# Moving the forget-gate log gathers of a two-layer hybrid decoder into the SSD tiles

## The chip, the cores and the metric

One Trainium2 chip, one core. The metric is the device time of one execution of the program in microseconds (us). Three executions of the kernel before took 2384.43, 2384.25 and 2366.11 us, median 2384.25 us. A further execution was recorded by the profiler and took 2400.34 us; its trace spans 2398.7 us from the first to the last instruction.

## The reference

The program computes one inference step of a two-layer decoder on 576 tokens: one new prompt of 512 tokens and eight running sequences with eight new tokens each. All numbers are 32-bit floats. In each layer a token mixer runs three branches on the same input, merges them with sigmoid gates, and projects:

```
u, q, k, v, fg, z, xbc, dt = split(x @ w_in)          # and three gates
logf  = log_sigmoid(fg + b)                           # forget gate, 8 heads
y_s5  = diagonal complex state space (u)
y_fox = softmax(q k' + cumulated logf differences) v  # forgetting attention
y_ssd = Mamba-2 state space (conv(xbc), dt)
out   = (g0*(y_s5 @ w0) + g1*(y_fox @ w1) + g2*(y_ssd @ w2)) @ w_o
```

For the running sequences the attention also reads a cache of 256 past tokens, held in pages of 128 tokens. For each sequence a page table names two pages, so 16 pages in all. The cache has keys, values (512 floats per token each) and the forget-gate logs `cache_logf` (8 floats per token). The score of a past token gets the sum of the forget-gate logs of all later past tokens, so the cached logs of all 16 pages are needed, once per layer, by the attention of the running sequences. After the mixer, layer 0 has a dense feed-forward part (width 2816) and layer 1 eight experts of which each token uses two.

## The kernel before

Everything is spread over five engines that run side by side, each in its own fixed order: TensorE (PE) for matrix products, VectorE (DVE) and ScalarE (ACT) for elementwise work, GpSimd (POOL) for elementwise work and for issuing transfers, and SyncE (SP), which issues the weight loads. A planner at build time puts the instructions of PE, DVE, ACT and POOL in order by a simulated timeline: an instruction goes to its engine once its inputs are ready there, and of several that are ready the one that stands first in the program. So work that stands late in the program is pulled forward into an engine's idle time if nothing holds it. SP's order is the order of the program (line 56). `tc.issue_after(x)` adds one constraint: what stands in the block comes behind `x` on `x`'s engine.

Every dense product is made exact by splitting each factor into a high and a low part: ACT rounds a weight tile (`wh`, line 97), DVE subtracts (`wl`, line 106), and PE multiplies three times (lines 294 to 296).

The order of the program in layer 0 (lines 1585 to 1598) is: load and transpose the input, issue the 16 log gathers of layer 0 (`gather_logs(0)`, line 1593), start the S5 constants (`s5_steps`, line 349), project `u`, then `mixer(0)`: the convolution, `ssd(0)`, keys, queries and values with the prompt's attention (`kqv_fox`), the S5 scan, and `fox_sample(0)`, the attention of the running sequences. Then come merge, output projection and the feed-forward part; `gather_logs(1)` stands in that part (line 1604), behind the S5 constants of layer 1.

`gather_logs` issues one indirect transfer per page from POOL (line 972). Each takes 128 rows of 8 floats into `lfp[:, i, :]`, with row numbers from `pgi`. The tile `lfp` has two buffers, one for each layer, so nothing makes the gathers of layer 1 wait for layer 0. They are read in `fox_sample` alone (line 1001): pair `bp` of sequences copies four of the 16 slices into `lq`, the left factor of a product.

`ssd(l)` walks over five tiles of tokens (four of 128 and one of 64) with a `front` and a `back` each. In a front, POOL loads the convolved input (`xc`, line 1158), multiplies `xd` by a decay into `xdd` (line 1169), and builds the masked decay matrices `ma` (line 1184; in layer 0 POOL builds the first of each pair and DVE the second). PE takes `ma` at line 1185 and `xdd` at line 1215. POOL's queue also holds, in the same stretch, the transfers of the prompt's attention (`kT`, `qT`, `vt`, `cb`, lines 890 to 900) and the subtractions for `kq` (line 859).

Of the kernel before, what the change touches and what calls it, by code (L numbers as in the profile page):

```python
# [8 lines left out]
F32 = mybir.dt.float32  # L9
# [10 lines left out]
P = 128  # L20
# [25 lines left out]
def decoder_step(ctx, tc, A, O):  # L46
    nc = tc.nc
    act, dve, pool, pe, sp = nc.scalar, nc.vector, nc.gpsimd, nc.tensor, nc.sync
    consts = ctx.enter_context(tc.tile_pool(name="consts", bufs=1))
    wk = ctx.enter_context(tc.tile_pool(name="wk", bufs=2))  # L50
# [9 lines left out]
    def U(tag, shape, dt=F32, name="u"):  # L60
        return cur["pool"].tile(shape, dt, name=name, tag=tag, bufs=cur["bufs"][tag])
# [4 lines left out]
    def SW(name="s"):  # L66
        return U("S", [P, 512], F32, name)

    def phase(name, **bufs):
        st_ = ExitStack()  # L70
        cur["pool"] = st_.enter_context(tc.tile_pool(name=name, bufs=1, reuse_waits="tile"))
        cur["bufs"] = bufs
        return st_
# [10 lines left out]
    def PX(name="px"):  # L84
        return ps.tile([P, 512], F32, name=name, tag="px", bufs=2)

    def PA(name="pa"):
        return ps.tile([P, 512], F32, name=name, tag="pa", bufs=1)
# [7 lines left out]
    def cp(out, in_):  # L96
        return act.activation(out, in_, AF.Copy)  # L97

    def mul(e, out, a, b):
        return e.tensor_tensor(out, a, b, op=OP.mult)  # L100

    def add(e, out, a, b):
        e.tensor_tensor(out, a, b, op=OP.add)  # L103
# [16 lines left out]
    def bc(ap, axis, n):  # L120
        u = ap.unsqueeze(axis)
        shp = list(u.shape)
        shp[axis] = n
        return u.to_broadcast(shp)
# [96 lines left out]
    pgi = []  # L221
# [9 lines left out]
    def tr(out, in_, n):  # L231
        pe.transpose(out, in_, ident[:n, :n])  # L232
# [3 lines left out]
    def x_dma(i):  # L236
        n = P if i < 4 else 64
        src = A["x_prompt"][0, i * P:(i + 1) * P, :] if i < 4 else A["x_sample"].rearrange("b t d -> (b t) d")
        xts[i] = xt = U("A", [P, D], name="xt")
        sp.dma_start(out=xt[:n], in_=src)  # L240

    def x_tr(i):
        n = P if i < 4 else 64
        xt = xts[i]
        for k0 in (0, 4):
            pt = (PX, PF)[k0 // 4]("xp")
            pv = pt.rearrange("p (k t) -> p k t", k=4)
            for k in range(4):
                tr(pv[:, k, :n], xt[:n, (k0 + k) * P:(k0 + k + 1) * P], n)
            s = slice(i * P, i * P + n)  # L250
            split(xh[:, k0:k0 + 4, s], xl[:, k0:k0 + 4, s], pv[:, :, :n])
# [6 lines left out]
    def wload(src, c0, ncol, kt, after=None):  # L258
        if WB["body"]:
            raw = [WB["pool"].tile([P, 4, P], F32, name="wb", tag="wb", bufs=2) for a in range(2)]  # L260
            for a in range(2):
                sp.dma_start(out=raw[a], in_=src[a * 512:a * 512 + 512, c0:c0 + P].rearrange("(k p) c -> p k c", p=P))
            return raw
        raw = wt_([P, 8, P], F32, "wr")
        i_ = sp.dma_start(out=raw[:, :kt, :ncol], in_=src[:, c0:c0 + ncol].rearrange("(k p) c -> p k c", p=P))
        if after is not None:
            tc.add_manual_dep(i_.ins, after.ins.name, mybir.DependencyInfo(
                mybir.DependencyClass.Sync, mybir.DependencyReason.DATA), reason="gather first")
        return raw
# [459 lines left out]
    def u_proj(l, hooks=(), first=()):  # L729
        us = {}  # L730

        def ev_u(j, h, o):
            if h == 0:
                us[j] = wk.tile([P, 8, 72], F32, name="us", tag="xp", bufs=4)
            ov = o.rearrange("p (k s) -> p s k", s=8)
            for a, b, k0 in (((0, 36, 8),), ((0, 28, 44), (28, 36, 0)))[h]:
                cp(us[j][:, :, k0:k0 + b - a], ov[:, :, a:b])
            if h == 1:
                i_ = pool.dma_start(out=UD[l][j * P:(j + 1) * P].rearrange("p (s k) -> p s k", s=8), in_=us[j])
                if j == 0:  # L740
                    S["late"] = i_
            for at, f in hooks:
                if (j, h) == at:
                    f()
        colblocks(A["w_in"][l], C_U, 512, 8, X, ev_u, by_half=True, first=first)
# [217 lines left out]
        for u_, r_ in pend:  # L963
            back(*u_, r_)

    lfps = {}

    def gather_logs(l):
        lfps[l] = lfp = wk.tile([P, 16, 8], F32, name="lfp", bufs=2)
        clf = A["cache_logf"].rearrange("l n p h -> (l n p) h")  # L970
        for i in range(16):
            pool.indirect_dma_start(out=lfp[:, i, :], out_offset=None, in_=clf,
                                    in_offset=bass.IndirectOffsetOnAxis(ap=pgi[l][:, i:i + 1], axis=0))

    def fox_sample(l):
        kS, qS, vn = S["kS"], S["qS"], S["vn"]
        lf = S["lf"]
# [97 lines left out]
    def conv(l, w_in):  # L1075
# [41 lines left out]
        for j0 in (0, 4):  # L1117
# [5 lines left out]
            pool.dma_start(out=O[7][l, 0, :, j0 * P:j0 * P + 512], in_=t_[0:3])  # L1123
            pool.dma_start(out=O[14][l].rearrange("b j c -> (b j) c")[:, j0 * P:j0 * P + 512], in_=t_[3:27])

    def ssd(l):
        lf = S["lf"]
        adt = wk.tile([P, 5, 8], F32, name="adt", bufs=1)
# [21 lines left out]
        v8 = lambda a: a.rearrange("p (h d) -> p h d", h=8)  # L1150
        st = {}

        def front(i):
            n = P if i < 4 else 64
            ts = slice(i * P, i * P + n)
            xc = [U(t_, [P, 512], name="xc").rearrange("p (j t) -> p j t", j=4)[:, :, :n] for t_ in ("S", "SR")]
            for q in range(2):
                pool.dma_start(out=xc[q], in_=XD[l][q * 4:q * 4 + 4].rearrange("j p t -> p j t")[:, :, ts])
            XC = lambda j: xc[j // 4][:, j % 4]
            mtri, mstr = (tri, strict_r) if i < 4 else (tri_b, strict_br)  # L1160
            es = ex[:, 1, i] if i < 4 else exs[:, 1]
            pt = PX()
            for j in range(4):
                tr(pt[:n, j * P:(j + 1) * P], XC(j), P)
            xdd, bt, yt = [U("SR", [P, 512], name=q) for q in ("xdd", "bt", "yt")]
            xd = SW("xd")
            mul(dve, v8(xd[:n]), v8(pt[:n]), bc(dt[:n, i], 2, 64))
            mul(dve, v8(yt[:n]), v8(pt[:n]), bc(tokp[l][:n, 24:32], 2, 64))
            mul(pool, v8(xdd[:n]), v8(xd[:n]), bc(es[:n], 2, 64))
            pt = PX()  # L1170
            for g in range(2):
                tr(pt[:n, g * P:(g + 1) * P], XC(4 + g), P)
                pe.matmul(pt[:n, 256 + g * P:256 + g * P + n], lhsT=XC(4 + g), rhs=XC(6 + g),
                          start=True, stop=True)
            cp(bt[:n, 0:256], pt[:n, 0:256])
            gm = bt[:n, 256:512].rearrange("p (g l) -> p g l", g=2)[:, :, :n]
            mul(dve, gm, pt[:n, 256:512].rearrange("p (g l) -> p g l", g=2)[:, :, :n], bc(mtri[:n, :n], 1, 2))
            yd = PA("yd")
            for g in range(2):
                pd = PX()  # L1180
                pdv = pd[:n].rearrange("p (h s) -> p h s", h=4)[:, :, :n]
                for a, (en, tg) in enumerate(((pool, "S"), ((pool, dve)[l == 0], "S"))):
                    ma = U(tg, [P, 512], F32R, name="ma")[:n].rearrange("p (h s) -> p h s", h=4)[:, :, :n]
                    mul(en, ma, bc(mtri[:n, :n], 1, 4), bc(ads[:n, a, i, g * 4:g * 4 + 4].bitcast(F32), 2, n))
                    pe.matmul(pdv, lhsT=mstr[:n, :n], rhs=ma, start=(a == 0), stop=(a == 1))
                mt = SW("mt")
                mtv = mt[:n].rearrange("p (h s) -> p h s", h=4)[:, :, :n]
                act.activation(mtv, pdv, AF.Exp)
                mul(dve, mtv, mtv, bc(gm[:, g], 1, 4))
                for h in range(4):  # L1190
                    c0 = (g * 4 + h) * 64
                    pe.matmul(yd[:n, c0:c0 + 64], lhsT=mtv[:, h, :], rhs=xd[:n, c0:c0 + 64], start=True, stop=True)
            add(dve, yt[:n], yd[:n], yt[:n])
            return XC, xdd, bt, yt
# [390 lines left out]
    with phase("mix0", **MA):  # L1585
        for i in range(3):
            x_dma(i)
        uw = [wload(A["w_in"][0], C_U + j * P, P, 8) for j in range(2)]
        for i in (3, 4):
            x_dma(i)  # L1590
        for i in range(3):
            x_tr(i)
        gather_logs(0)
        s5g = s5_steps(0)
        u_proj(0, (((0, 0), lambda: x_tr(3)), ((1, 0), lambda: x_tr(4)), ((0, 1), lambda: next(s5g)),
                   ((1, 1), lambda: params_dma(0)), ((2, 1), lambda: next(s5g)), ((3, 1), lambda: params_tr(0)),
                   ((3, 1), lambda: next(s5g))), uw)
        mixer(0)
# [439 lines left out]
```

## Time and profile before

| what | us |
|---|---|
| median of three executions | 2384.25 |
| lowest and highest of them | 2366.11, 2384.43 |
| profiled execution | 2400.34 |
| span of its trace | 2398.7 |
| PE busy | 2277.4 (95% of the span) |
| DVE busy | 1573.7 (66%) |
| ACT busy | 1134.5 (47%) |
| POOL busy | 560.4 (23%) |

Busy time is the time in which an engine executes; issuing a transfer on SP is not counted as busy. Idle time of an engine is put down to what ended it: another engine's instruction, a transfer (DMA), or "issue", which means that the engine waited for nothing that the trace shows. Line 232 is the transpose helper, lines 97, 100, 103, 106 and 109 are helpers for elementwise work, so tiles rather than lines tell these apart. A time such as 20.48 is counted from the start of the span.

### The profile page before, as it was taken

What the parts mean: (1) busy time and instruction counts of PE and PEld (TensorE: products, weight loads), DVE (VectorE), ACT (ScalarE), POOL (GpSimd) and SP (SyncE); (2) the same over time, 40 slices, a digit from 0 to 9 for tenths busy, and PEclk for the clock granted to TensorE, in tenths of its full rate; (3) what the DMA queues carried; (4) which work ended last, traced back from release to release, by engine and by line L of the source; (5) the groups of instructions that cost most, each with busy time, mean ns of one, the idle gap of its engine ahead of it and who ended that gap; (6) DMA issues with size and microseconds to landing.
All of it is one profiled execution on the core that took longest, in us unless ns stands there. A gap on an engine that the chain in (4) does not pass through costs nothing. (4 is left out here: it accounts for less than half of the span.)

```text
span 2398.7 us, 45369 instructions
## 1 busy us (share of the span) xinstructions
PE 2277.4 (95%) x17037; PEld 2158.2 (90%) x17038; DVE 1573.7 (66%) x3725; ACT 1134.5 (47%) x2538; POOL 560.4 (23%) x712
## 2 busy tenths in 40 slices
PE   5999999998999999999999999899999699999995
PEld 5899997888998999999899998789999599999995
DVE  4956687556588843334765697456447578888886
ACT  2354443453346323223644443354334467777773
POOL 6733224333130110001124324233003310101000
PEclk7999999999999999999999999899999799999997
DMA  5566556856445432233576557757333799999993
GB/s 125 174 177 206 160 155 186 202 160 215 118 126 157 147 96 83 80 89 103 139 188 184 157 152 195 186 156 211 89 99 108 199 229 255 255 253 259 236 258 100
DMA packets 587436, 399.91 MB, mean 167 GB/s; under 512 B 59436, under 2 KB 548188, under 8 KB 587176
## 3 DMA queue, kind: packets, MB, share of 16 engines
q1 hardware_dynamic: 475272, 236.30, 37.2%
q0 software_dynamic: 30912, 95.12, 14.4%
q10 hardware_dynamic: 81024, 65.51, 9.5%
q8 instruction: 136, 2.23, 0.4%
q14 instruction: 92, 0.75, 0.1%
HBM read 326.02 MB, written 70.92 MB: 165 GB/s over the span
## 5 line engine op out<-in xcount | busy, mean ns | idle before, releaser
L106 DVE TENSOR_TENSOR wl<-wr,wh 128x512 fp32r<-128x512 f32 x886 | 629.1, 719 | 364.0 <-ACT wh L97 346.6
L97 ACT ACTIVATE wh<-wr 128x512 fp32r<-128x512 f32 x886 | 549.0, 625 | 511.0 <-PE mm L295 364.9
L294 PE MATMUL mm<-xh,wh 128*128 128x288 f32 (+1 forms) x2048 | 617.8, 302 | 15.3 <-issue 7.9
L295 PE MATMUL mm<-xl,wh 128*128 128x288 f32 (+1 forms) x2048 | 613.9, 300 | 7.9 <-issue 5.2
L296 PE MATMUL mm<-xh,wl 128*128 128x288 f32 (+1 forms) x2048 | 612.8, 299 | 5.1 <-issue 4.4
L294 PEld LDWEIGHTS mm<-xh,wh 128*128 128x128 f32 (+1 forms) x2048 | 386.3, 189 | 26.0 <-issue 11.6
L295 PEld LDWEIGHTS mm<-xl,wh 128*128 128x128 f32 (+1 forms) x2048 | 386.1, 189 | 17.1 <-issue 10.9
L296 PEld LDWEIGHTS mm<-xh,wl 128*128 128x128 f32 (+1 forms) x2048 | 385.8, 188 | 13.1 <-issue 9.8
L1788 PE MATMUL mm<-xe,wh 128*128 128x352 f32 x448 | 134.3, 360 | 1.8 <-issue 1.8
L1788 PE MATMUL pf<-xe,wh 128*128 128x352 f32 x448 | 132.2, 358 | 0.5 <-issue 0.5
L1789 PE MATMUL mm<-xe,wl 128*128 128x176 f32 x512 | 118.0, 251 | 1.8 <-issue 1.8
L1789 PE MATMUL pf<-xe,wl 128*128 128x176 f32 x512 | 117.6, 250 | 1.5 <-issue 1.5
L294 PE MATMUL mm<-hq,wh 128*128 128x288 f32 x352 | 104.3, 296 | 0.2 <-DVE rf L103 0.2
L294 PE MATMUL pf<-xh,wh 128*128 128x288 f32 x352 | 104.3, 296 | 0.0
L296 PE MATMUL mm<-hq,wl 128*128 128x288 f32 x352 | 104.2, 296 | 0.0
L296 PE MATMUL pf<-xh,wl 128*128 128x288 f32 x352 | 104.1, 296 | 0.0
L295 PE MATMUL pf<-xl,wh 128*128 128x288 f32 x352 | 103.8, 295 | 0.0
L295 PE MATMUL mm<-hq,wh 128*128 128x288 f32 x352 | 103.7, 295 | 0.0
L1789 PEld LDWEIGHTS mm<-xe,wl 128*128 128x128 f32 x512 | 97.9, 194 | 1.6 <-issue 1.6
L1789 PEld LDWEIGHTS pf<-xe,wl 128*128 128x128 f32 x512 | 97.2, 193 | 0.5 <-issue 0.5
L1788 PEld LDWEIGHTS mm<-xe,wh 128*128 128x128 f32 x448 | 86.5, 193 | 2.4 <-issue 2.4
L1337 ACT ACTIVATE gt<-mm,prm 128x288 f32<-128x288 f32 x96 | 47.4, 494 | 85.4 <-PE mm L296 75.1
(662 smaller groups left out, 5310.4 us busy)
## 6 DMA issues: line engine op xcount, KB each, us to landing
wr<-in_w_in_dram SPq DMA_DIRECT2D x108, 512.0 KB
wr<-in_moe_w_gate_dram SPq DMA_DIRECT2D x64, 512.0 KB
wr<-in_moe_w_up_dram SPq DMA_DIRECT2D x64, 512.0 KB
wr<-in_moe_w_down_dram SPq DMA_DIRECT2D x64, 512.0 KB
wr<-in_w_o_dram SPq DMA_DIRECT2D x32, 512.0 KB
wr<-in_ffn_w_gate_dram SPq DMA_DIRECT2D x25, 512.0 KB
wr<-in_ffn_w_up_dram SPq DMA_DIRECT2D x25, 512.0 KB
wr<-in_ffn_w_down_dram SPq DMA_DIRECT2D x24, 448.0 KB
```

Source lines behind the costliest of these rows:

```text
L97: return act.activation(out, in_, AF.Copy)
L106: e.tensor_tensor(out, a, b, op=OP.subtract)
L294: pe.matmul(o, lhsT=wh_[:, a, :m], rhs=x[0][:, k, s], start=(st and k == 0), stop=False)
L295: pe.matmul(o, lhsT=wh_[:, a, :m], rhs=x[1][:, k, s], start=False, stop=False)
L296: S["mm"] = pe.matmul(o, lhsT=wl_[:, a, :m], rhs=x[0][:, k, s], start=False, stop=(sp_ and k == kt - 1))
L1337: act.activation(t[h], o[h], AF.Tanh, scale=0.5, bias=prm[l][:, c0:c0 + 1])
L1788: pe.matmul(o, lhsT=h_[:, k % 4, :], rhs=xf, start=(k == 0), stop=False)
L1789: pe.matmul(o[:, 0:CAP], lhsT=l_[:, k % 4, :], rhs=x[:, k, 0], start=False, stop=False, skip_group_check=True)
```

## The change

The 16 gathers of layer 0 leave the start of the program. They stand in `ssd(0)` instead, four in each of the first four token tiles, directly behind the product `xdd` on POOL. `gather_logs(1)` stays where it was in the program. The tile `lfp` now has one buffer, so layer 1's gathers can be issued only when layer 0's last reader at line 1001 is through.

```diff
-    def gather_logs(l):
-        lfps[l] = lfp = wk.tile([P, 16, 8], F32, name="lfp", bufs=2)
...
-        for i in range(16):
+    def gather_logs(l, i0=0, i1=16):
+        if i0 == 0:
+            lfps[l] = wk.tile([P, 16, 8], F32, name="lfp", bufs=1)
+        lfp = lfps[l]
...
+        for i in range(i0, i1):
             pool.indirect_dma_start(out=lfp[:, i, :], out_offset=None, in_=clf,
                                     in_offset=bass.IndirectOffsetOnAxis(ap=pgi[l][:, i:i + 1], axis=0))
...
     def ssd(l):
...
-            mul(pool, v8(xdd[:n]), v8(xd[:n]), bc(es[:n], 2, 64))
+            i_ = mul(pool, v8(xdd[:n]), v8(xd[:n]), bc(es[:n], 2, 64))
+            if l == 0 and i < 4:
+                with tc.issue_after(i_.ins):
+                    gather_logs(0, 4 * i, 4 * i + 4)
...
         for i in range(3):
             x_tr(i)
-        gather_logs(0)
         s5g = s5_steps(0)
```

## Rows read from the trace of the kernel before

**Rows 1.** The page: span, and each engine's busy us, share and instructions.

```profile
span 2398.7 us, 45369 instructions
PE 2277.4 (95%) x17037; PEld 2158.2 (90%) x17038; DVE 1573.7 (66%) x3725; ACT 1134.5 (47%) x2538; POOL 560.4 (23%) x712
```

**Rows 2.** Busy time by stretch: engines' us (instructions), PE's clock share, DMA, GB/s.

```profile
20.50:40.20 19.70, 3.35 (x11) 2.11 (x9) 0.00 (x0) 0.00 (x0) 11.99 (x13) 0.60 0.30 63
40.20:48.40 8.20, 8.20 (x39) 7.77 (x40) 6.29 (x40) 4.28 (x12) 3.99 (x6) 0.50 0.19 20
...
200.00:300.00 100.00, 99.04 (x772) 92.06 (x771) 61.52 (x111) 44.95 (x108) 34.70 (x41) 1.00 0.62 179
...
510.00:560.00 50.00, 50.00 (x462) 46.30 (x462) 24.09 (x48) 17.21 (x35) 13.03 (x21) 1.00 0.67 199
...
740.00:1100.00 360.00, 360.00 (x2766) 358.55 (x2765) 184.77 (x414) 120.49 (x238) 15.12 (x23) 1.00 0.35 104
```

**Rows 3.** The gathers and their readers: ns min/median/max, first and last start.

```profile
L972 POOL DMA_INDIRECT lfp<-in_cache_logf_dram,pgi x32: 948/952/1339, 5.7 to 87.3; - x32
L1001 DVE COPY lq<-lfp x32: 175/186/737, 341.8 to 1595.7; 128x64 f32<-128x64 f32 x32
```

**Rows 4.** POOL in order of time, start of the program: start, duration, instruction, idle before.

```profile
35.20 0.95 POOL L972 DMA_INDIRECT lfp<-in_cache_logf_dram,pgi  x1 [0.31 <-issue]
...
59.00 0.95 POOL L972 DMA_INDIRECT lfp<-in_cache_logf_dram,pgi  x1 [0.30 <-issue]
...
66.26 5.04 POOL L457 COPY bbd<-s5b 64x256 f32<-64x256 f32 x3 [4.56 <-DMA lfp<-in_cache_logf_dram,pgi]
```

**Rows 5.** PE in order of time, from 20 to 50 us.

```profile
20.48 0.29 PE L296 MATMUL mm<-xh,wl 128*128 128x288 f32 x1
22.60 0.29 PE L294 MATMUL mm<-xh,wh 128*128 128x288 f32 x1 [1.83 <-issue]
...
49.56 0.29 PE L296 MATMUL mm<-xh,wl 128*128 128x288 f32 x1
49.69 0.29 PE L294 MATMUL mm<-xh,wh 128*128 128x288 f32 x1
```

**Rows 6.** SP's issues of the parameter loads: layer 0, then layer 1.

```profile
22.57 0.73 SPq L713 DMA_DIRECT2D prow<-in_ln_g_dram  x1
...
37.35 2.10 SPq L265 DMA_DIRECT2D wr<-in_w_in_dram  x2
...
707.88 0.55 SPq L713 DMA_DIRECT2D prow<-in_b_gate_dram  x1
...
713.46 0.43 SPq L715 DMA_DIRECT2D tokp<-in_ssd_d_dram  x1
```

**Rows 7.** PE's waits for POOL: 60 to 150 us, then 510 to 720 us.

```profile
PE p L232 <- POOL bm L103: 1.9, 1, 1.9
...
PE px L1263 <- POOL lns L103: 4.1, 1, 4.1
```

**Rows 8.** POOL in order of time in the SSD tiles: the third tile.

```profile
245.82 1.04 POOL L100 TENSOR_TENSOR xdd<-xd,ex 128x512 f32<-128x512 f32 x1 [5.29 <-DVE xd L100]
246.82 1.49 POOL L100 TENSOR_TENSOR ma<-tri,ads 128x512 fp32r<-128x512 f32 x1
```

**Rows 9.** PE in order of time in the same tile.

```profile
249.56 0.39 PE L1185 MATMUL px<-ma,br 128*128 128x512 f32 x1
```

**Rows 10.** The fourth tile: POOL's last `ma`, then PE's products that take it.

```profile
286.88 1.05 POOL L100 TENSOR_TENSOR ma<-tri,ads 128x512 fp32r<-128x512 f32 x1
...
292.22 0.62 PE L1185 MATMUL px<-ma,br 128*128 128x512 f32 x2
```

**Rows 11.** The gathers of key and value pages: ns min/median/max, first and last start.

```profile
L1011 POOL DMA_INDIRECT kpg<-in_cache_k_dram,pgi x32: 942/1000/2025, 422.5 to 1602.6; - x32
L1037 POOL DMA_INDIRECT vpg<-in_cache_v_dram,pgi x32: 941/976/1641, 353.4 to 1615.9; - x32
```

**Rows 12.** DVE in order of time: the last reader of layer 0's log tile.

```profile
507.96 1.04 DVE L1001 COPY lq<-lfp 128x64 f32<-128x64 f32 x4
```

More of the change, by code (lines that the diff above doesn't have):

```diff
@@ L964, in lag @@
             back(*u_, r_)
-    lfps = {}
-    def gather_logs(l):
-        lfps[l] = lfp = wk.tile([P, 16, 8], F32, name="lfp", bufs=2)
-        clf = A["cache_logf"].rearrange("l n p h -> (l n p) h")
-        for i in range(16):
-            pool.indirect_dma_start(out=lfp[:, i, :], out_offset=None, in_=clf,
-                                    in_offset=bass.IndirectOffsetOnAxis(ap=pgi[l][:, i:i + 1], axis=0))
     def fox_sample(l):
@@ L1124, in conv @@
             pool.dma_start(out=O[14][l].rearrange("b j c -> (b j) c")[:, j0 * P:j0 * P + 512], in_=t_[3:27])
+    lfps = {}
+    def gather_logs(l, i0=0, i1=16):
+        if i0 == 0:
+            lfps[l] = wk.tile([P, 16, 8], F32, name="lfp", bufs=1)
+        lfp = lfps[l]
+        clf = A["cache_logf"].rearrange("l n p h -> (l n p) h")
+        for i in range(i0, i1):
+            pool.indirect_dma_start(out=lfp[:, i, :], out_offset=None, in_=clf,
+                                    in_offset=bass.IndirectOffsetOnAxis(ap=pgi[l][:, i:i + 1], axis=0))
     def ssd(l):
```

## The prediction, made before the changed kernel ran

> **What bounds the kernel now.** I read the page first: PE is busy for 2277.4 of 2398.7 us, and POOL, the engine that the change touches, for 560.4 [rows 1]. So work that moves on POOL counts only where PE waits, directly or through another engine. The view by stretches then shows where PE is not full. From 200 to 300 us, where the gathers go, PE works 99.04 of 100 us and POOL 34.70; from 510 to 560 and from 740 to 1100 us PE has no gap and POOL stands idle for 37 and 345 us [rows 2]. The waits of PE for POOL are two in the first 720 us, 1.9 and 4.1 us, and neither lies in the SSD tiles [rows 7].
>
> The exception is the start, where the gathers lie now. The view by tile shows 32 of them, 0.952 us each, from 5.7 to 87.3 us: layer 1's sixteen are pulled up to the start as well [rows 3]. In the order of time 24 of them are issued back to back up to 35.20 us, each with 0.3 us ahead of it, seven more up to 59.00 us and one at 87.3 us [rows 4]. And from 20.50 to 40.20 us PE is held: 11 products in 19.70 us, with gaps of 1.83 us and the like between them and nothing as the cause but "issue"; DVE and ACT execute nothing [rows 2, 5]. SP is slow in the same stretch: its last twelve parameter loads take from 22.57 to the next weight load at 37.35 us, while layer 1's thirteen take 6 us at 708 us, where POOL issues no gathers and PE is not held [rows 6].
>
> **The change, part by part.** The sum is made on the profiled execution, 2400.3 us, which is 16.1 us above the median of the three timed ones; a difference is carried over to the median as it is.
>
> *Start, without the hold.* 32 gathers of 0.95 and 0.3 us leave POOL, 40 us in all, and with them one wait: behind the gather of 59.00 us, POOL stood 4.56 us at `bbd` until a log transfer had landed [rows 4]. This chain of S5 constants meets PE once, in the 1.9 us that PE waited for `bm` [rows 7]. Ends: 0 and -4.6. I take -1.9, because that row is the only one where POOL's lateness there reaches PE.
>
> *The hold.* It costs 19.70 us less 11 products at the usual 0.13 us (49.56 to 49.69 [rows 5]), so 18.3 us, and PE then works 39 products at a clock share of 0.50, the lower of its two levels (1.2 GHz), which loses about 3 us more [rows 2]. No row says what causes it. Two readings are left. If the gathers on POOL cause it together with SP's many small loads, it goes with them. If it is an event of the start, or of the recording, it stays where it was or was never in the timed runs. For the first speaks that layer 1 has the same loads without gathers and without a hold [rows 6]. For the second speaks that gathers run from 5.7 us on without a hold until 20.5, and a last seven up to 59 us where PE is not held [rows 2, 4, 5], that POOL's own issue keeps its pace in the hold, and that the profiled execution is longer than the median by 16.1 us, about one hold, so that the median may well have none. I take 0; the other end is the first rival's.
>
> On this the Trainium skill, DMA: Bandwidth & Descriptors, section SWDGE vs HWDGE vs iDMA, says that POOL writes its descriptors into rings in SBUF and that transfers issued from SP never touch that path. By it the gathers would not be what slows SP, and the start would give the 0 to -4.6 us above and no more; the slow SP in the hold is a row that the rule leaves unexplained.
>
> *SSD tiles of layer 0.* Sixteen gathers come into POOL's queue, four of them, 5.0 us, behind each `xdd` (4 times 0.952 and 0.3). POOL has room: 65 us idle of 100, against 20 us [rows 2]. What counts is what stands right behind. In the third tile `ma` follows `xdd` at once, ends at 248.3, and PE takes it at 249.56, so 1.3 us to spare [rows 8, 9]; in the fourth it ends at 287.9 and is taken at 292.22, 4.3 us to spare [rows 10]. If the gathers get between, PE is 3.7 us late in the third tile and 0.7 in the fourth, and as much again in the first two at the most of these two figures (0.7 to 3.7 each): 5.8 to 11.8 us. If the planner, which counts the gathers, puts `ma` first or gives PE a product in between, it is 0. Its orders are made from ready times, and `ma` needs no loaded input, so it is often ready before `xdd`. I take +1. The gathers themselves may be slower beside a busy DVE (61.52 of 100 us [rows 2]): page gathers in such stretches have medians of 0.976 and 1.000 us and a longest of 2.025 [rows 11], so at worst 16 us more on POOL, which its idle time holds. Their data is first wanted at 341.8 us [rows 3], some 50 us after the fourth tile's `ma`: a late landing costs 0.
>
> *Layer 1.* With one buffer its gathers wait for the last reader in layer 0's attention, which ends at 509 us [rows 12]; then 20.0 us of issue must find a place. The 37 us idle up to 560 us hold them, and the 345 us of the feed-forward part hold them seventeen times [rows 2]. They are first wanted in layer 1's attention, which is over 1000 us off. What can be late is what POOL issues behind them in the merge, up to the 4.1 us wait of PE for `lns` [rows 7]. Ends 0 and +20 (all sixteen in front of that `lns`, 1.25 each). I take 0. The buffer that goes and the later place in the code cost nothing by themselves: same instructions, same bytes.
>
> Sum: -1.9 + 0 + 1 + 0 = -0.9, so 2399.4 us on the profiled execution and 2383 us on the median. This case, **small terms only**, reaches from -6 to +10: 2378 to 2394 us.
>
> **Rivals.** *The hold goes with the gathers.* PE then gains 18.3 and 3 us, and gives some back: SP would issue the third weight at about 27 us instead of 37.35 (6 us for the parameters [rows 6] from 20.5), it was in use some 10 us later, at 37 us, and PE's remaining 59 products end at about 30 (by 0.13 us each [rows 5], with some transposes). So about 7 us are lost again by the wait for weights, at most; 14 to 21 us are won, with the small terms 15 to 24. I take 17: 2367 us. Speaking for it besides [rows 6]: the timed runs of this one kernel lie 18.3 us apart (2366.11 and 2384.43), as if the hold came in some and not in others.
>
> *A train of gathers ahead of work that PE wants next* makes the kernel slower. The place is POOL's queue, in the SSD tiles behind `xdd` and in the merge ahead of `lns`. It decides where the planner puts a train of four (5.0 us) in front of an instruction whose spare time is less, such as the 1.3 us at 248.3 [rows 8, 9]. Price: 5.8 to 11.8 us in layer 0 and up to 20 in layer 1; I take 8 and 10, with the -1.9 of the start +16: 2400 us. Against it: POOL is idle two thirds of that time, and the planner knows of the gathers.
>
> *It doesn't do what it says.* `issue_after` only says "not before". All orders are planned anew, and gathers may end up late, for instance just ahead of the reader at 341.8 us, where each group that PE waits for costs up to its 5.0 us: 4 times 5.0, or 2403 us, at worst; half of that, 2393 us, as its middle.
>
> **Numbers.** Chances: small terms 0.46, hold gone 0.30, train 0.18, planned otherwise 0.06. The predicted time is that of the first, 2383 us. The range of 8 in 10 goes from 2360 us (of the second case about a quarter lies below, 0.08) to 2402 us (of the third about half lies above and some of the fourth, 0.11). A change of over 1% of the median, 23.8 us, is about what a measurement can tell from none. Faster than 2360.4 us: a third of the second case and a trace of the first, 0.12. Slower than 2408.1 us: a third of the third and some of the fourth, 0.08. Within: 0.80.
>
> **What would show it.** In the changed kernel's trace no gather should stand before 200 us; four each should follow the `xdd` of the first four tiles, and sixteen come after 510 us. If PE still makes one product in 2 us between 20 and 40 us, the hold is not the gathers'; if such 11 products take 1.5 us, it was. The wait of `bbd` for a log transfer should be gone. In the SSD tiles, PE waiting for POOL's `ma` would mean the train; PE's wait for `lns` near 589 us longer than 4.1 us would mean it for layer 1. I am wrong in kind if the time moves by more than the named terms while none of these rows differs, for then it is the new plan of all orders that does it.

## The result and the profile after

The changed kernel took 2394.44 us in the median (2385.91 to 2403.15, 16 runs), the kernel before, on the same chip, 2383.19 us (2366.11 to 2392.63, 16 runs). The medians lie 11 us apart; the ratio is 1.006, with an interval of 1.0044 to 1.0076: some 14 us slower (10 to 18). The forecast was 2383 us, a change of almost nothing, so it is 11 us too low. The time lies within the range and within the 1% that had most of the chance, at the upper end of the case "small terms only" (2394 us).

The profiled execution of the changed kernel took 2394.63 us, and its page begins so (answers to [rows 1]):

```profile
span 2393.0 us, 45353 instructions
PE 2279.9 (95%) x17037; PEld 2160.2 (90%) x17038; DVE 1573.5 (66%) x3725; ACT 1135.4 (47%) x2538; POOL 556.6 (23%) x712
```

This is 5.7 us less than the profile before, while the timed runs are longer. So the profile before can't be set beside it as it is. Its hold of 19.7 us [rows 2, 5] is the main reason: two more profiles of the same kernel (below, before_again and before_third) have none. In the view by stretches, from 20.5 to 40.2 us, PE works 17.33 us in the third profile of the kernel before, gathers and all, and 18.46 us in the changed kernel; the profile before had 3.35.

```profile
20.50:40.20 19.70, 17.33 (x124) 17.03 (x124) 12.39 (x89) 8.07 (x24) 15.23 (x18) 0.91 0.54 123
```

```profile
20.50:40.20 19.70, 18.46 (x133) 18.16 (x132) 13.12 (x94) 8.12 (x24) 4.84 (x7) 0.91 0.67 164
...
200.00:300.00 100.00, 100.00 (x790) 92.70 (x789) 62.07 (x118) 47.30 (x116) 47.34 (x53) 1.00 0.60 171
```

**The gathers went where the prediction put them.** By tile and in the order of time (answers to [rows 3, 4]) there are none before 195.8 us, four groups of four behind `xdd`, and the last ends near 530 us; `bbd` no longer waits for a log transfer:

```profile
L1125 POOL DMA_INDIRECT lfp<-in_cache_logf_dram,pgi x32: 944/952/1295, 195.8 to 529.7; - x32
```

```profile
41.34 1.06 POOL L457 COPY bbd<-s5b 64x256 f32<-64x256 f32 x2 [0.28 <-DVE s5a L103]
```

**Where the time went.** The two kernels do the same products in a different order, so times of day can't be compared directly. I added up the columns that PE's matmuls stream, instruction by instruction, and looked for the moments at which each kernel had streamed as much as the third profile of the kernel before had at 16.5, 44, 131, 201, 341, 517.5 and 619.6 us. Between two such moments PE does the same amount of work. Five of these stretches, in the kernel before (third profile) and then in the changed kernel; the columns are those of [rows 2]:

```profile
16.50:44.00 27.50, 25.13 (x185) 24.83 (x184) 19.68 (x122) 9.98 (x28) 21.81 (x25) 0.94 0.59 121
44.00:131.00 87.00, 81.39 (x643) 76.36 (x641) 65.25 (x123) 31.40 (x63) 61.97 (x64) 0.98 0.71 198
201.00:341.00 140.00, 139.43 (x1067) 128.52 (x1067) 99.98 (x249) 62.69 (x153) 39.65 (x50) 1.00 0.58 162
341.00:517.50 176.50, 167.96 (x1237) 139.13 (x1237) 106.97 (x313) 76.92 (x193) 62.23 (x83) 0.92 0.68 174
517.50:619.60 102.10, 94.32 (x757) 91.45 (x756) 61.92 (x120) 37.24 (x72) 29.96 (x50) 0.95 0.61 187
```

```profile
17.70:44.20 26.50, 25.26 (x185) 24.96 (x184) 18.70 (x113) 10.04 (x28) 7.76 (x12) 0.93 0.75 183
44.20:138.10 93.90, 84.10 (x643) 78.89 (x641) 68.30 (x125) 31.25 (x64) 53.22 (x53) 0.95 0.59 167
208.00:346.70 138.70, 138.70 (x1065) 128.06 (x1064) 101.39 (x261) 63.17 (x154) 51.03 (x60) 1.00 0.60 166
346.70:517.90 171.20, 164.64 (x1217) 137.88 (x1216) 106.94 (x302) 77.10 (x190) 66.87 (x88) 0.94 0.68 178
517.90:632.20 114.30, 98.22 (x777) 93.37 (x777) 60.68 (x118) 38.59 (x74) 40.13 (x61) 0.94 0.57 171
```

The reader should take the second number of each line, the length. The S5 constants grow by 6.9 us, the SSD tiles shrink by 1.3, the S5 scan with the attention shrinks by 5.3, the merge grows by 12.2. From 632 us on the two differ by 2 us (the changed kernel is the shorter). Each kernel has one profile, the kernel before three, so these lengths are those of single executions. The same for every profile of this case:

```
length in us of the same PE work    start  S5 const.  SSD    scan+att.  merge
before (first profile, with hold)    45.8    84.1    140.4    170.1     101.0
before_again                         25.9    86.0    140.0    178.1     101.9
before_third                         27.5    87.0    140.0    176.5     102.1
after                                26.4    93.9    138.7    171.2     114.3
l0_only                              26.5    93.6    141.5    188.9     102.7
l1_only                              26.6    96.5    140.8    169.8     114.3
after_l1_late                        28.7    93.0    138.9    171.6     102.4
l1_behind_keys                       26.8    93.1    138.9    171.9     107.9
l1_behind_values                     26.7    93.9    138.7    170.1     111.9
l1_behind_zs                         25.6    94.3    138.7    170.0     113.3
late_plus_start                      26.0    83.2    138.8    169.4     102.5
both_start                           26.7    82.3    140.2    178.2     100.7
bm_later                             25.2    94.3    138.7    171.5     102.3
bm_third                             25.4    78.6    139.0    171.0     103.5
```

Against the mean of the two profiles before without the hold (26.7, 86.5, 140.0, 177.3, 102.0) the changed kernel's terms are -0.3, +7.4, -1.3, -6.1 and +12.3, together +12.0, inside the 10 to 18 us of the timed runs. The terms that repeat are the merge, 100.7 to 103.5 us in the nine profiles without layer 1's gathers in it and 107.9 to 114.3 in the five with them, and the S5 constants, 93 us or more only in kernels that have fewer than 32 gathers at the start. The scan does not repeat: the kernel before has 170.1, 178.1 and 176.5 us there.

**The merge.** PE's waits in the last stretch, before (third profile) and after (answers to [rows 7]; us in total, times, longest):

```profile
PE px L1263 <- POOL lns L103: 4.5, 1, 4.5
PE mm L294 <- DVE gt L109: 2.9, 1, 2.9
```

```profile
PE px L1268 <- POOL lns L103: 5.5, 1, 5.5
PE mm L294 <- DVE gt L109: 4.5, 3, 3.6
PE mm L294 <- ACT gt L1342: 3.3, 1, 3.3
PE px L232 <- DMA kpg<-in_cache_k_dram,pgi: 2.4, 1, 2.4
```

The 2.4 us for the key pages are new. POOL's queue in the changed kernel shows why: the sixteen gathers of layer 1 start as soon as the log tile is free, and fourteen of them stand ahead of the key pages of the last pair of sequences:

```profile
507.84 0.94 POOL L1125 DMA_INDIRECT lfp<-in_cache_logf_dram,pgi  x1 [0.30 <-DVE yl L106]
...
524.51 0.95 POOL L1125 DMA_INDIRECT lfp<-in_cache_logf_dram,pgi  x1 [0.30 <-issue]
525.77 0.95 POOL L1002 DMA_INDIRECT kpg<-in_cache_k_dram,pgi  x1 [0.30 <-issue]
...
538.04 1.01 POOL L1028 DMA_INDIRECT vpg<-in_cache_v_dram,pgi  x1 [3.84 <-PE pa L1024]
...
554.21 1.15 POOL L1416 DMA_DIRECT2D yft<-FD  x2 [7.51 <-DMA FD<-yfs]
```

The last pair ends late, its result reaches the merge's load `yft` late, and PE runs out of other products one wait after the other, down to `lns`. PE is idle for 16.1 us of this stretch instead of 7.8, which is 8.3 of the 12.2 us; for the rest it works longer, at a clock share of 0.94 instead of 0.95 and on 777 instructions instead of 757. In the kernel before the same key page went out at 503.78 us (third profile).

**The S5 constants.** PE's waits from 44 to 131 us before (third profile), and from 44.2 to 138.1 us after:

```profile
PE mm L296 <- DVE wl L106: 2.9, 2, 1.5
PE p L232 <- POOL bm L103: 1.9, 1, 1.9
```

```profile
PE mm L296 <- DVE wl L106: 5.6, 2, 4.3
PE p L232 <- DVE kz L109: 2.4, 1, 2.4
PE mm L294 <- ACT gt L1342: 1.7, 1, 1.7
```

PE no longer waits for POOL's `bm`, as forecast, but for DVE: for a low part `wl` and for `kz`. And the clock is lower, 0.95 against 0.98. Of the 6.9 us, 4.2 are PE's idle time (9.8 less 5.6) and 2.7 longer work.

### The profile page after: what moved, and what is told of

It is laid out like the page before. It is cut to its first block, busy times and chain, and to the rows that moved or that the text cites. A ratio compares the mean times of both kernels' runs of the same rounds, so it can differ in the third digit from the quotient of the medians.

```text
span 2393.0 us, 45353 instructions
## 1 busy us (share of the span) xinstructions
PE 2279.9 (95%) x17037; PEld 2160.2 (90%) x17038; DVE 1573.5 (66%) x3725; ACT 1135.4 (47%) x2538; POOL 556.6 (23%) x712
```

## The experiments

Times are medians, ratios against the kernel before measured beside them on the same chip, in three groups (2380.74, 2378.80 and 2380.02 us). "Behind x" means `tc.issue_after` on x.

**Half of the change each, and layer 1 later.** before_again is the kernel before without an edit.

> The kernel before, unchanged, profiled once more. If the hold from 20.5 to 40.2 us belongs to the kernel (to the gathers at the start), it is there again: PE busy below 6 of 20 us between 20 and 40 us, span about 2399 us. If it was an event of one execution, PE is busy for more than 15 of these 20 us, and the span is about 2380 us. In the second case this trace is the one to set beside the changed kernel's, whose span of 2393.0 us is then about 13 us longer, and the place of these 13 us can be read.

It took 2384.79 us, span 2383.1 us, and PE was busy for 17.67 us from 20.5 to 40.2 us. The hold was an event of one execution; of fourteen profiles in this case one has it.

```
l0_only:    lfps[l] = wk.tile([P, 16, 8], F32, name="lfp", bufs=2)    # after, was bufs=1
l1_only:    lfps[l] = lfp = wk.tile([P, 16, 8], F32, name="lfp", bufs=1)    # before, was bufs=2
after_l1_late:
-        gather_logs(1)
         ffn()
+        with tc.issue_after(S["xs"].ins):      # the last xsum on POOL
+            gather_logs(1)
```

> Only the other half: layer 0's 16 gathers at the start as before, one buffer, so that layer 1's gathers come after layer 0's attention has read its logs, near 510 us. Theory T: +8 to +14 us, 2391 to 2397 us, with PE waiting for the last pair's key pages as in the changed kernel (2.4 us) and the merge late. Theory S: no loss or half of it, 2383 to 2388 us, since half of the gathers are at the start. Theory P: anything between -10 and +12 us.

2397.89 us, ratio 1.0070 (1.0049 to 1.0092): theory T, just above its range. The merge takes 114.3 us, as in the changed kernel to the tenth, with the same train of fourteen. But the start is as bad as there, 96.5 us, with half of the gathers still in it, which theory S had put at half the loss or none. The profiled execution took 2410.29 us, 12 us more than the median, and its part behind the merge, where nothing was edited, is 11 us longer than in the third profile of the kernel before.

> Only the first half of the change: layer 0's gathers in the SSD tiles, two buffers, so that layer 1's gathers are free to run early (they come right behind the first group of four). Theory T (the 14 gathers of layer 1 ahead of the last pair's page gathers, near 510 us, cost the time): no loss, 2383 us, within 4 us of the kernel before. Theory S (the start without gathers is worse, because the S5 constants' work on POOL now meets other work on DVE): about +10 us, 2393 us. Theory P (any new plan moves the time by some 10 us): anything between -10 and +12 us.

2399.41 us, ratio 1.0088 (1.0064 to 1.0112). No theory's number, some 21 us (15 to 27) above the kernel before: the merge is fine (102.7, as T says), the start is bad (93.6, as S says), and the scan and attention are 11.6 us longer than before. There PE waits 7.8 us for ACT's copy `kk` and 4.7 us for key pages, in an order that no other kernel has; what in that plan brings `kk` late I did not follow up. This run speaks for theory P, that a new plan alone can cost 10 us, but nothing here separates the plan from the 32 gathers that it has in the SSD tiles.

> The changed kernel with layer 1's 16 gathers held behind the last POOL sum (xsum) of the feed-forward part, near 900 us, where POOL is idle. Theory T: the loss near 510 to 600 us goes, 2381 to 2386 us. Theory S: it stays, 2391 to 2396 us. If both hold in part, in between, and the stretches tell how much is whose: T is the shift between 340 and 620 us, S the one up to 120 us.

2383.48 us, ratio 1.0016 (0.9995 to 1.0036). With the gathers at 880 to 900 us the merge takes 102.4 us: the 12 us are the train's. Key pages go out at once, 0.88 us after the value page before them:

```profile
506.59 0.96 POOL L1028 DMA_INDIRECT vpg<-in_cache_v_dram,pgi  x1 [0.30 <-issue]
508.42 0.95 POOL L1002 DMA_INDIRECT kpg<-in_cache_k_dram,pgi  x1 [0.88 <-DVE zt__6458 L109]
```

The loss of the start stays (93.0), and the gain in the scan (171.6) about pays for it.

**Where in the merge the train hurts.** The same line with other instructions in place of `S["xs"]`: the last `kpg` gather of layer 0, the last `vpg` gather, the last load of `zs`.

> The changed kernel with layer 1's 16 gathers held behind the last key page gather (kpg) of layer 0's attention instead of 14 ahead of it: the train still starts near 515 us and now stands ahead of the last two value pages (vpg), which the changed kernel issued at 538 us. Theory T1 (what costs is the last pair's key pages, delayed by the train): most of the 12 us between 520 and 620 us is won back, 2383 to 2387 us, PE's wait for the key pages under 1 us. Theory T2 (any train in POOL's queue between 507 and 570 us delays the merge by its own length): nothing is won, 2391 to 2396 us; PE then waits for the value pages or for lns.

2389.58 us, ratio 1.0031 (1.0008 to 1.0054), between the two theories' ranges; merge 107.9 us, half of the loss. PE's waits there:

```profile
PE px L1268 <- POOL lns L103: 4.5, 1, 4.5
PE po L1052 <- DMA vpg<-in_cache_v_dram,pgi: 3.4, 1, 3.4
```

> The same with the 16 gathers behind the last value page gather (vpg), so that they stand in groups of 9 and 7 among the loads of the gates (gt) ahead of the merge. Theory T1: all won back, 2381 to 2385 us. Theory T2: the loss stays or moves to the loads of gt and yft, 2388 to 2396 us.

2393.47 us, ratio 1.0056 (1.0036 to 1.0077); merge 111.9 us. Now PE waits for the gates whose loads (`gt<-GD`) stand between and behind the gathers:

```profile
PE mm L294 <- DVE gt L109: 14.7, 4, 5.8
```

> The same with the 16 gathers behind the last load of zs, the place named in the prediction (in the merge, around the additions of lns that PE waits for). If a train there costs what the prediction's rival said, PE's wait for lns grows from 4.1 us to 8 us or more and the time is 2388 to 2400 us. If the gathers slip into POOL's idle time between the additions, the wait stays under 5 us and the time is 2381 to 2386 us.

2401.47 us, ratio 1.0077 (1.0046 to 1.0107); merge 113.3 us. The wait for `lns` is what the prediction's rival had described, in two pieces:

```profile
PE px L1268 <- POOL lns L103: 13.5, 2, 9.4
```

T1 alone falls: behind the value pages it had 2381 to 2385 us. T2 holds in kind and not in size: wherever the twenty microseconds of gathers stand between 507 and 581 us, something that PE wants next is behind them, and only its name changes (key pages, value pages, gates, `lns`). In the merge the price goes from 5.9 to 12.3 us, not the train's whole length; and ahead of the value pages it is half of that ahead of the key pages. The profile of l1_behind_zs is 8 us longer behind the merge as well, where nothing was edited.

**What the start lost.** late_plus_start is after_l1_late with 32 more gathers at the start, into a tile that nobody reads.

```
+        for l in range(2):
+            lfd = wk.tile([P, 16, 8], F32, name="lfd", bufs=2)
...
+                pool.indirect_dma_start(out=lfd[:, i, :], out_offset=None, in_=clf,
+                                        in_offset=bass.IndirectOffsetOnAxis(ap=pgi[l][:, i:i + 1], axis=0))
         s5g = s5_steps(0)
```

> The changed kernel with layer 1's gathers behind the feed-forward sums, and with 32 more gathers at the start into a tile that nobody reads, as many as the kernel before has there. Theory S1 (the start lost 8 to 10 us because POOL, freed of its gathers, runs its S5 work earlier beside DVE): the loss up to 200 us against the kernel before goes from +8 to within 2 us. Theory S2 (the start differs by the new plan alone): it stays between 5 and 12 us. Theory G (the loss of the start is given back before 520 us whatever it is, because the S5 scan waits for something else there): the whole time stays within 4 us of the kernel before in either case; without G, S1 gives a kernel about 8 us faster, 2375 us.

2370.04 us, ratio 0.9959 (0.9939 to 0.9980): 40 us of useless work on POOL make it faster than both kernels. The S5 constants take 83.2 us instead of 93.0, even 3.3 less than in the kernel before, and nothing of it is given back later; S2 and G fall. The rows of that stretch, in after_l1_late and in late_plus_start:

```profile
44.70:137.70 93.00, 82.61 (x643) 77.32 (x642) 67.47 (x125) 31.27 (x64) 52.76 (x54) 0.96 0.60 169
```

```profile
43.90:127.10 83.20, 79.64 (x634) 75.45 (x633) 65.20 (x126) 31.44 (x63) 58.54 (x67) 1.00 0.75 210
```

DVE's busy time falls by 2.3 us only. The 9.8 us are PE's idle time (3.6 us instead of 10.4) and a clock share of 1.00 instead of 0.96. So S1's result came, but the sum of its reason, DVE's work made longer beside POOL's, is a small part of it; the rest is when that work is due for PE.

```
both_start:    gather_logs(0)
              +gather_logs(1)          # and none in the feed-forward part
bm_later:     +with nullcontext() if l or q else tc.issue_after(S["ud"].ins):      # 4th store of u
                   cmul(dve if l else pool, bm[:, 0], bm[:, 1], ...)
bm_third:      for i in range(2):      # layer 0, instead of cmul
                   mul(pool, bm[:, i], pr_[:, :, 0:8], bc(bb[:, i, gs], 2, 8))
```

both_start is an edit of the kernel before, the other two are edits of after_l1_late. bm_third leaves out four of the six POOL operations of each `bm` of layer 0, so it is there to measure with and is no version to use.

> A version meant to beat both: the kernel before (two buffers), with layer 1's 16 gathers written right behind layer 0's at the start, so that all 32 go out in one row and nothing of them is left for the SSD tiles or the merge. If the gain of the previous experiment came from the 32 gathers that keep POOL off its S5 products until about 47 us, the first 130 us run as there, the merge has no train, and the time is 2368 to 2376 us. If it came from something else in that plan (the gathers in the SSD tiles), the time is that of the kernel before, 2378 to 2384 us.

2377.80 us, ratio 0.9995 (0.9975 to 1.0015). The start is as short as hoped (82.3 us), but scan and attention take 178.2 us as in the kernel before, where late_plus_start has 169.4. So the gain of that experiment had two sources, and this version has one of them; it can't be told from the kernel before.

> As after_l1_late, but of the six POOL operations that form each bm of layer 0 only two are done (the two products without the cross terms: that part of the S5 constants is left out). Theory C: DVE's operations between 43 and 90 us are no longer stretched (ef in 0.2 us each, its row of 14 instructions in under 10 us instead of 15), and the stretch that took 93.0 us takes 80 to 86. Theory Q: 90 to 95 us, as DVE has the same work.

2368.28 us, ratio 0.9953 (0.9934 to 0.9971). What C says of the durations is so. The stretch takes 78.6 us, and PE has no gap in it:

```profile
43.20:121.80 78.60, 78.60 (x642) 74.77 (x642) 51.56 (x126) 31.27 (x64) 27.18 (x38) 1.00 0.72 204
```

DVE executes 126 instructions there, against 125 in after_l1_late, in 51.56 us instead of 67.47. The same instructions in after_l1_late and here, two of the row of `ef` (start, duration):

```profile
73.65 1.20 DVE L109 SCALAR_TENSOR_TENSOR ef<-ef,ab 128x80 f32<-128x80 f32 x1
...
76.26 2.32 DVE L135 TENSOR_SCALAR ef<-ef 128x80 f32<-128x80 f32 x1
```

```profile
66.33 0.24 DVE L109 SCALAR_TENSOR_TENSOR ef<-ef,ab 128x80 f32<-128x80 f32 x1
...
66.88 0.20 DVE L135 TENSOR_SCALAR ef<-ef 128x80 f32<-128x80 f32 x1
```

In the first kernel POOL works on `bm` and `s5u` and issues two transfers meanwhile, in the second it stands idle:

```profile
73.64 1.11 POOL L100 TENSOR_TENSOR s5u<-s5a,s5b 128x512 f32<-128x512 f32 x1
...
76.69 1.18 POOL L100 TENSOR_TENSOR s5u<-s5a,s5b 128x512 f32<-128x512 f32 x1
77.74 0.81 POOL L497 DMA_DIRECT2D BD<-bo  x1
```

The low part `wl` that PE waits for is queued behind this row on DVE. That does not yet tell the changed kernel from the kernel before. DVE works 65.25 us in this stretch of the third profile, against 68.30 in the changed kernel, and its operations on `ef` alone (the rows below: the length of the stretch, then DVE's time on that tile alone) take longer in before_again than in the changed kernel:

```profile
43.80:129.80 86.00, 14.71 (x15) 0.98 0.72 204
```

```profile
44.20:138.10 93.90, 12.32 (x15) 0.95 0.59 167
```

So the stretching is in both kernels. Which of DVE's instructions it hits, and whether PE has other products then, differs with the planned order, and between these two Q is not refuted.

> The changed kernel with layer 1's gathers behind the feed-forward sums (as in after_l1_late, no gathers at the start), and the first POOL products of the S5 constants (bm of the first quarter) held behind the fourth store of u, near 51 us instead of 44. Theory C (POOL's two-input products slow DVE beside them, and DVE is what PE waits for at the start): the stretch of PE's work that took 93.0 us there and 84 to 86 in the kernel before takes 87 to 91 us, and the DVE products ca between 43 and 50 us last 0.75 us instead of 1.0 to 1.7; the whole time falls by 2 to 6 us. Theory Q (the start differs by the planned order of DVE alone, its instructions being as fast): no change of these durations, 92 to 95 us.

2383.95 us, ratio 1.0011 (0.9992 to 1.0031), as without the edit. The DVE products `ca` do last 0.75 us, as C says (the first three in after_l1_late together 3.21), but the stretch takes 94.3 us: the overlap only moved. The row of `ef` begins 2 us earlier and then meets the same POOL work. C is right about the durations; the length is what Q had, and my price for this one delay was wrong.

> The kernel before, profiled a third time, to see how often its first 520 us hold a disturbance. The two profiles so far had one each: the hold (19.7 us) and a stretch of 20.5 us at half clock in the S5 scan (8 us). If such events are common, a third profile has one again and spans 2378 to 2400 us; if they are rare, it has none and spans about 2372 to 2378 us, and the sum of the changed kernel's three terms (start +9, SSD tiles -1.5, merge +12.5) should show in full.

2384.10 us, span 2382.5 us. No hold, but the event in the scan again. PE waits 3.1 us for a transfer at 388.5 us (`p<-uc,tu`), and then works for 19.4 us at a clock share of 0.50, its lower level of 1.2 GHz:

```profile
388.00:391.60 3.60, 0.48 (x5) 0.27 (x4) 1.80 (x4) 0.30 (x2) 0.00 (x0) 0.88 1.00 297
391.60:411.00 19.40, 19.40 (x66) 14.28 (x67) 6.63 (x19) 3.61 (x9) 0.85 (x2) 0.50 0.29 77
```

Five of the fourteen profiles have such a wait of 3.1 to 3.6 us in one piece. In three of them (before_again, before_third, both_start) some 20 us at the lower level follow at once, and the stretch takes 176.5 to 178.2 us; in two the clock stays (the first profile of the kernel before) or is at the lower level for 3.4 us only (l1_only), and it takes 170.1 and 169.8. The changed kernel's order has no such wait at that place. It has its own time at the lower level, behind shorter waits for `tu` and `cu` near 430 us:

```profile
430.00:451.00 21.00, 18.60 (x81) 15.91 (x81) 10.12 (x27) 6.69 (x19) 4.52 (x7) 0.52 0.63 149
```

So the shorter stretch has two sources, by the rows of the result: PE is idle for 6.6 us (171.2 less 164.6) instead of 8.5, and a clock share of 0.94 instead of 0.92 is worth 10.3 us (0.06 of 171.2) instead of 14.1. How often either kernel has this event in the timed runs no profile shows, so of all terms this one is the least certain. It is likely too large: the two profiles without the hold span 2383.1 and 2382.5 us, while the 72 timed runs of the kernel before, in the three groups, have a mean span of 2378 us at a mean clock share of 0.973, and the 16 of the changed kernel 2393 us at 0.971. Over its whole length the changed kernel has no more of the full clock than the kernel before.

## Why the prediction was right or wrong, point by point

The time fell where the range and the chances had it, but not by the steps that I gave: of the four terms two failed, and in the profiles a gain that no step had made up for half of one. That the range held is in this part luck.

**The step that failed is "Layer 1".** It said that the 37 us of idle POOL up to 560 us hold the gathers, and took 0 between 0 and +20. They cost 12.3 us, and moving them to 880 us gives these back (after_l1_late, 102.4 us). POOL is idle there because its transfers wait for the last pair of the attention, one after the other, not because there is room: a busy share says how much work an engine has, not how soon its next instruction is wanted. The rival with the train had the mechanism, 10 us for layer 1 and its place among others at `lns`; the place was the key pages, 60 us earlier, which [rows 11] had listed without my asking what is queued behind the train there. So the sign that I gave, a longer wait for `lns`, grew by 1.0 us only (5.5 against 4.5). l1_behind_zs shows that the place named would have cost about as much.

**"Start, without the hold".** I took -1.9 between 0 and -4.6; it is +7.4. Two things happened as written: the wait of `bbd` went, and PE's wait for `bm` too. What failed is the bound "0": I counted only the one row in which PE waits for POOL, and took POOL's gathers for a load only. In the changed kernel PE waits longer for DVE (`wl`, `kz`) and has less of the full clock. That POOL's S5 products stretch DVE's instructions there, and that the stretch is shorter by 14 us without two thirds of them, is shown by bm_third; that 32 gathers at its start shorten it by 10 us, by late_plus_start and both_start. That the second comes from the first is not shown: with the gathers DVE is busy for 65.20 us, without them for 67.47. They also change the order that the planner makes, and which of the two counts stays open, as does why 16 gathers (l1_only, 96.5 us) are no better than none.

On this the Trainium skill, SBUF — State Buffer, section Who interferes with whom, has the rule that I should have weighed: a DVE instruction with two inputs in SBUF contends with a GpSimd instruction that reads SBUF, for port pairs that only one of them can hold at a time. The traces agree: `ef<-ef,ab` takes 1.20 us beside POOL's products and 0.24 us without them. The 2.32 us of `ef<-ef` are outside that sentence, as it has one input, and no run here shows what held it. The section also says that such a DVE instruction does not contend with a GpSimd instruction that only writes SBUF, and infers that a tensor_tensor and the writing of descriptors don't meet; here `ca` takes 0.75 us beside the gathers of late_plus_start, as it does beside an idle POOL.

**"The hold".** 0 was right. It is in no other profile, neither with gathers at the start (before_again, before_third, both_start) nor without. The first rival, with a chance of 0.30, falls; what held PE and SP in that one execution stays open.

**"SSD tiles of layer 0".** I took +1, measured -1.3. In the changed kernel PE has no gap from 200 to 300 us, and none of its waits up to 345 us is for POOL. In all four tiles the four gathers stand between `xdd` and the next `ma` on POOL. The third tile, as feared (answers to [rows 8, 9], POOL and then PE):

```profile
232.51 1.04 POOL L100 TENSOR_TENSOR ma<-tri,ads 128x512 fp32r<-128x512 f32 x1 [1.87 <-PE yd L1197]
236.30 1.04 POOL L100 TENSOR_TENSOR xdd<-xd,ex 128x512 f32<-128x512 f32 x1 [2.75 <-DVE xd L100]
237.50 1.29 POOL L1125 DMA_INDIRECT lfp<-in_cache_logf_dram,pgi  x1 [0.15 <-issue]
...
245.33 1.18 POOL L100 TENSOR_TENSOR ma<-tri,ads 128x512 fp32r<-128x512 f32 x1
```

```profile
251.69 0.73 PE L1190 MATMUL px<-ma,br 128*128 128x512 f32 x2
```

That `ma` ends at 246.5 us, and PE, which has other products up to then, takes it 5.2 us later. It is the case "gives PE a product in between". Here this half of the change is free.

**What no step had.** The scan's -6.1 us against two of the three profiles of the kernel before: a wait of 3 us that the new order hasn't, and less time at the lower clock. Against the first, which has the wait and keeps the clock, it is +1.1. The prediction's last sentence left this way open (the new plan of all orders); its rival "doesn't do what it says" had 2393 us, but by late gathers ahead of their reader, and none was late.

So the sum was -1.9 + 0 + 1 + 0, and is +7.4 + 0 - 1.3 + 12.3, with -6.1 for the scan in these profiles.

## What to carry to other kernels

An engine that is idle for most of a stretch may still be the one that every next step passes through: before moving a train of transfers there, list what is queued behind it and when PE takes it. Work that is taken off an engine lets its other work start earlier, beside other work of its neighbours, and changes the planned order of all; cost the removal like an addition. And before a difference is explained, profile the kernel before a second time: here the first profile held 19.7 us that no other profile has.

## What the runs showed of the hardware

A two-input DVE operation of 0.24 us lasted 1.20 us beside POOL's two-input products, and one of 0.20 us with one input lasted 2.32 us while POOL ran such a product and issued two transfers. 126 DVE instructions took 51.56 us, instead of 67.47 for 125, when two thirds of these products were left out: almost a quarter of DVE's busy time there went with them. An indirect gather on POOL (0.95 us, and 0.30 between two) did not stretch DVE's products beside it (0.75 us).

The time of one execution follows the granted clock: over the 26 runs of the kernel before in the second group, spans go from 2367 us at a mean clock of 0.979 to 2391 us at 0.969, and 0.010 of some 2380 us is 24 us, the whole difference between the two. Most of the kernel's scatter of 1% goes with how long PE runs at its lower level.
